# One decoder layer with a product-key expert mixer on one core: slot sums, one-hots and projection order changed

## The chip, the cores and the metric

The program runs on one core of a Trainium2 chip, in one launch. The metric is the device time of that launch in microseconds (us). An engine is named as the profile names it: TensorE is PE (matmuls) and PEld (its weight loads), VectorE is DVE, ScalarE is ACT, GpSimd is POOL, and SyncE (SP) only issues transfers.

## What is computed

The layer runs on 1024 prompt tokens and 64 sample tokens of width 1024, all in float32. Tokens lie in tiles of 128 rows: tiles 0 to 7 are the prompt, tile 8 (64 rows) is the sample group. Gating and retention heads, a cross-attention into 256 memory tokens and the expert mixer follow one another, each with a residual and a layer norm. The mixer is what the change is about, cut here to its core:

```python
q = (xt @ wq).reshape(128, 8, 2, 128)                      # 8 heads, two halves
s = einsum('thcd,hckd->thck', q, subkeys)                  # 128 keys per half
sv, si = top_k(s, 16)
cand = sv[:, :, 0, :, None] + sv[:, :, 1, None, :]         # 256 candidates per head
fv, fi = top_k(cand, 16)                                   # 8 x 16 = 128 experts per token
g = softmax(fv)
act = gelu(einsum('thed,td->the', u_tab[eidx], xt))
f = einsum('the,thed->td', g * act, v_tab[eidx])           # tables of 16384 x 1024
```

## The kernel before

**Two ways through the mixer.** Tiles 1, 2, 3, 4 (`DT`) go the dense way: every expert of the tables is projected for them, in 128 blocks of 128 experts, and a table of weights that is zero nearly everywhere picks the chosen ones. Tiles 0, 8, 5, 6, 7 (`GT`) go by gathers: POOL issues one indirect transfer for each of the 128 slots of a tile (L1154, L1157), which brings one row of 1024 numbers for each of up to 128 partitions into `gbuf` (7 buffers).

**Gathers.** The list `jobs` is written from `JORD`: `u` is a slot whose rows of the first table are dotted with the tokens by DVE (L1087), into one column of `hd`. The values come in two forms. In form `v` a gather fetches the 128 rows of one token, and PE sums them with 32-column matmuls into `cb` (L1128): two matmuls for a gather, four records in the profile. In form `w` a gather fetches one slot for all tokens, and DVE adds it, scaled by a column of `hd`, to the sum `fo` (L1099). Before the change only tile 7, which is last, has form `w`; tile 0 is first in the list and has form `v`.

**The front.** `front()` sends four batches of tiles ([0], [1, 2, 8], [3, 4, 5], [6, 7]) through the projections; all of their large matmuls are L148, into `mm`. While PE projects for one batch, the route of the batch before (`post_peer`) selects its experts, mostly on DVE (L617 to L661). For a tile of the dense way the selection ends in 32 groups of one-hots (`onehots`): `oi` marks one half index (DVE, L705), `oj` the other one, already times the weight (ACT, L702 and L703, two instructions for each of 4 rows), PE multiplies the two (`gb`, L719), ACT copies the product into the one buffer `big` (L720), and after every fourth group SP stores it to `gsc` in DRAM (L723). One tile at a time does this.

**The dense part.** `do_h(i)` projects block i (24 matmuls, L973), ACT takes the gelu (L977), DVE multiplies by the stored table `G` (L980), and hi and lo parts go to `ah` and `al`. Then 48 matmuls for two blocks (L1024) add their values `vh`, `vl` into `oa` to `od`. The first two blocks are projected while the last selections still run; then the pools of the selection close (`qctx.close()`), two pools for values and sums open in their place, and the rest follows.

**What sets the order.** Two generators, the front with the dense part and the gathers, each have a clock that its yields advance; the one that is behind is asked next, and its clock gives its instructions their priority. A scheduler then fixes one order for each engine, which the chip follows strictly: an instruction that waits holds up all that stand behind it on its engine, a transfer on SP's or POOL's queue too.

Of the kernel before, what the change touches and what calls it, by code (L numbers as in the profile page):

```python
# [13 lines left out]
AF = mybir.ActivationFunctionType  # L14
ALU = mybir.AluOpType
# [39 lines left out]
SPREAD = (0,1,2,3)  # L55
HEAD = "w_o w_o + wq wq + wo wo + pq pq + pq pq + +"
PIN = 1
PO = 0
PG = 0
PC = 0  # L60
PP = 0
# [7 lines left out]
ND = 2  # L69
GT = [0,8,5,6,7]  # L70
DT = [1,2,3,4]
JORD = ("u0","v0","u8","v8","u5","v5a","u6 v5b","u7 v6","w7")
FB = 2
COST_G = 1.4
COST_F = 1.1
# [83 lines left out]
def body(ctx: ExitStack, tc: tile.TileContext, a):  # L159
    nc = tc.nc  # L160
# [40 lines left out]
    iota = C("iota")  # L201
# [58 lines left out]
    def pin(x, PIN=1):  # L260
        if not PIN:
            return
        n = 0
        for i in reversed(nc.cur_bb.bb.instructions):
            if i is not x.ins and i.engine == x.ins.engine and i.name not in low:
                n += 1
                if n == PIN:
                    tc.add_manual_dep(x.ins, i.name, mybir.DependencyInfo(mybir.DependencyClass.NoSync,
                                                                          mybir.DependencyReason.DATA), reason="order")
                    return  # L270
# [317 lines left out]
    def post_peer(t, c, p, sub):  # L588
# [26 lines left out]
        for j in range(4):  # L615
            x = s[:P, j * 128:(j + 1) * 128]
# [68 lines left out]
        if c == 3 and dn:  # L685
            while st.get("gsl") or not st.get("gok"):
                yield
            st["gsl"] = True
            tp = GB()
            for j, src in enumerate((eid[:, 0, :], eid[:, 1, :], gw)):  # L690
                nc.tensor.transpose(tp[:, j * 128:(j + 1) * 128], src, ident)
            kt = TQ([128, 5, 128], "kt", 1)
            tpv = tp[:, :384].rearrange("p (a b) -> p a b", a=3)
            nc.scalar.activation(kt[:, :3, :], tpv, AF.Copy)
            nc.scalar.activation(kt[:, 3:5, :], tpv[:, 1:3, :], AF.Copy, scale=-1.0)
            yield
            n = DT.index(t)

            def onehots(g):
                oj = TQ([128, 4, 128], "oj", OJ)  # L700
                for r in range(4 * g, 4 * g + 4):
                    nc.scalar.activation(oj[:, r % 4, :], iota, AF.Abs, bias=kt[:, 3, r:r + 1])  # L702
                    nc.scalar.activation(oj[:, r % 4, :], oj[:, r % 4, :], AF.Relu, bias=kt[:, 2, r:r + 1], scale=kt[:, 4, r:r + 1])  # L703
                oi = TQ([128, 4, 128], "oi", OI)
                x = nc.vector.tensor_tensor(oi, iota.unsqueeze(1).to_broadcast([128, 4, 128]),  # L705
                                            kt[:, 0, 4 * g:4 * g + 4].unsqueeze(2).to_broadcast([128, 4, 128]), op=ALU.is_equal)
                pin(x, PO)
                return oi, oj

            nxt = onehots(0)  # L710
            for g in range(32):
                if g % 4 == 0:
                    gs = TQ([128, 128, 16], "big")
                oi, oj = nxt
                if g < 31:
                    nxt = onehots(g + 1)
                g4 = GB()
                for r in range(4):
                    nc.tensor.matmul(g4[:, r * 128:(r + 1) * 128], lhsT=oj[:, r, :], rhs=oi[:, r, :], start=True, stop=True)  # L719
                nc.scalar.activation(gs[:, :, g % 4 * 4:g % 4 * 4 + 4].rearrange("p i t -> p t i"),  # L720
                                     g4.rearrange("p (t i) -> p t i", t=4), AF.Copy)
                if g % 4 == 3:
                    nc.sync.dma_start(gsc[8 * n + g // 4], gs)  # L723
                if g % 2:
                    yield
            st["gsl"] = False
        elif c == 3:
            tp = GB() if XG else SM()
            nc.tensor.transpose(tp[:, :P], eid[:P, 0, :], ident[:P, :P])
            nc.vector.tensor_copy(done["ixT", t][:, :P], tp[:, :P])  # L730
            done["v", t] = True
            if t == SMP:
                for x in (done["ix", t], gw):
                    nc.sync.dma_start(x[64:, :64], x[:64, 64:])
                done["u", t, 3] = True
# [166 lines left out]
    def dense():  # L902
# [6 lines left out]
        def TE(shape, tag, bufs=1, dt=F32):  # L909
            return pe[0].tile(shape, dt, name=tag, tag=tag, bufs=bufs)  # L910
# [10 lines left out]
        NB = 128  # L921
# [3 lines left out]
        def load_u(i):  # L925
            if i < NB:
                raw["u", i] = TD([128, 8, 128], "ur", ND)
                nc.sync.dma_start(raw["u", i], a["Ud"][i])

        def load_v(i):  # L930
            if i < NB:
                raw["v", i] = TE([128, 1024], "vr", ND)
                nc.sync.dma_start(raw["v", i], a["V"][i * 128:(i + 1) * 128, :])

        def load_g(q):
# [6 lines left out]
        def split_u(i):  # L942
            if i < NB:
                h, l = TD([128, 8, 128], "uh", 2, F32R), TD([128, 8, 128], "ul", 2, F32R)
                split(h, l, raw.pop(("u", i)))
                Uw[i] = (h, l)
                load_u(i + ND)
# [13 lines left out]
            del r  # L961
        for i in range(ND):
            load_u(i)
        split_u(0)
        split_u(1)
        A = {}

        def do_h(i):
            h, l = Uw.pop(i)
            p = pp.tile([128, nd * 128], F32, name="h", tag="h", bufs=2)  # L970
            for k in range(8):
                for j, (w, x) in enumerate(((h, xh), (h, xl), (l, xh))):
                    nc.tensor.matmul(p, lhsT=w[:, k, :], rhs=x[:, k, :], start=k == 0 and j == 0, stop=k == 7 and j == 2)  # L973
                if k % 2 and k < 7:
                    yield 1.35
            ga = TD([128, nd * 128], "ga", 2)
            nc.scalar.activation(ga, p, AF.Gelu_apprx_tanh)  # L977
            gv = ga.rearrange("p (h g t) -> p h g t", h=2, t=16)
            for j in range(2):
                nc.vector.tensor_tensor(gv[:, j], gv[:, j], Gb[i // 8, j][:, :, i % 8, :], op=ALU.mult)  # L980
            ah, al = TD([128, nd * 128], "ah", 2 * FB, F32R), TD([128, nd * 128], "al", 2 * FB, F32R)
            split(ah, al, ga)
            A[i] = (ah, al)
            if i % 8 == 7:
                del Gb[i // 8, 0], Gb[i // 8, 1]
                load_g(i // 8 + 1)
# [2 lines left out]
            step_all()  # L989
            yield 1.0  # L990
        load_g(0)
        for i in range(FB):
            yield from do_h(i)
            split_u(i + 2)
            step_all()
            yield 1.35
        while active:
# [2 lines left out]
        qctx.close()  # L1000
        pe = [ctx.enter_context(tc.tile_pool(name="pe", bufs=1, side="right")),
              ctx.enter_context(tc.tile_pool(name="po", bufs=1, space=bass.MemoryType.PSUM, side="right"))]
        for i in range(ND):
            load_v(i)
        for t in DT:
            y = TE([128, 1024], "acc", nd)
            nc.sync.dma_start(y, done["x2", t])
# [2 lines left out]
            split_v(i)  # L1010
        phase[0] = 2
        for f in range(NB // FB):
            for i in range((f + 1) * FB, (f + 2) * FB):
                if i < NB:
                    yield from do_h(i)
                    split_u(i + 2)
                    yield 1.35
            for n, t in enumerate(DT):
                o = [O(2 * (n % 2) + j) for j in range(2)]
                for b in range(FB):  # L1020
                    i = f * FB + b
                    for ia, iv in ((0, 0), (0, 1), (1, 0)):
                        for j in range(2):
                            nc.tensor.matmul(o[j], lhsT=A[i][ia][:, n * 128:(n + 1) * 128],  # L1024
                                             rhs=Vw[i][iv][:, j * 512:(j + 1) * 512],
                                             start=b == 0 and ia + iv == 0, stop=b == FB - 1 and ia == 1)
                    if b < FB - 1:
                        yield 1.4
                for j in range(2):
                    y = acc[n][:, j * 512:(j + 1) * 512]  # L1030
                    nc.vector.scalar_tensor_tensor(y, y, ALPHA if f == 0 else 1.0, o[j], op0=ALU.mult, op1=ALU.add)
                if f == NB // FB - 1:
                    if n == 0:
                        lg, lb = TE([128, 1024], "vr", ND), TE([128, 1024], "vr", ND)
                        nc.sync.dma_start(lg, bc(a["ln3_g"], 1024))
                        nc.sync.dma_start(lb, bc(a["ln3_b"], 1024))
                    finish(acc[n], t, lg, lb)
                if n == nd - 1:
                    for b in range(FB):
                        del A[f * FB + b], Vw[f * FB + b]  # L1040
                        split_v((f + 1) * FB + b)
                yield 1.4

    def main():
        yield from front()
# [192 lines left out]
```

## Time and profile before

| | |
|---|---|
| median of 3 runs | 3679.9 us (3675.48 to 3682.37) |
| the profiled execution | 3672.27 us, span 3670.5 us |
| mean granted TensorE clock | 0.931 of full speed |
| busy share | PE 88%, PEld 56%, DVE 68%, ACT 35%, POOL 49% |
| chain that ended last | PE 63%, DVE 13%, DMA 9% |
| first and last `h` matmul start | 2044.1 us, 3630.2 us |

The shares are means over stretches that differ. The front ends and the dense part begins at about 2044 us; the rows below go by stretches, cut where PE passes from one part of the front to the next.

### The profile page before, as it was taken

The page shows a single profiled execution, that of the slowest core. Times are in us where ns is not written, and L with a number is a line of the kernel's source. Part 1 is how long each engine was busy: PE and PEld are TensorE (multiplying, and loading weights), DVE is VectorE, ACT ScalarE, POOL GpSimd, SP SyncE. Part 2 cuts the span into 40 slices and gives each one's busy share as a digit, 9 for nine tenths or more (in the row PEclk, how much of TensorE's full clock was granted, in tenths as well). Part 3 has the DMA queues.
Part 4 walks back from the last instruction along what each step waited for, and adds up shares of the span by engine and source line. Part 5 has one row for each costly group of instructions (what it writes and reads, how often), then busy time and mean ns, then how long its engine had stood idle before and what let it go on. Part 6 is the DMA issues. An engine that isn't in the chain of part 4 may idle for free.

```text
span 3670.5 us, 41634 instructions
## 1 busy us (share of the span) xinstructions
PE 3244.9 (88%) x13368; PEld 2037.7 (56%) x13368; DVE 2496.5 (68%) x5941; ACT 1274.3 (35%) x2634; POOL 1784.9 (49%) x1427
## 2 busy tenths in 40 slices
PE   8999558889997899984789779999999999999998
PEld 3444223333445554442445467777777777788886
DVE  2135874325678622799858769878877777799996
ACT  1121211112238785231677932222322322322222
POOL 0013575234546633446744546555565655566631
PEclk9989679899998899986889889999999999999999
DMA  8747677778768887667888879988999989898872
GB/s 271 258 158 275 214 285 278 253 268 283 269 235 330 309 307 283 210 235 263 300 308 313 305 275 338 327 306 316 337 332 347 343 317 324 298 322 318 309 239 75
DMA packets 407354, 1039.67 MB, mean 283 GB/s; under 512 B 37280, under 2 KB 129632, under 8 KB 403040
## 3 DMA queue, kind: packets, MB, share of 16 engines
q0 software_dynamic: 165888, 604.05, 45.3%
q1 hardware_dynamic: 229392, 420.06, 33.5%
q10 hardware_dynamic: 11856, 12.91, 1.0%
q8 instruction: 105, 1.72, 0.2%
q14 instruction: 113, 0.93, 0.1%
HBM read 985.59 MB, written 51.25 MB: 282 GB/s over the span
## 4 chain that ended last, share of the span: by engine, by line
PE 63%; DVE 13%; DMA 9%; POOL 5%; issue 5%; ACT 5%; SPq 0%; POOLq 0%; DVEq 0%; ACTq 0%
PE mm L148 20%; PE h L973 15%; PE cb L1128 5%; PE oa L1024 4%; PE oc L1024 4%; PE od L1024 4%; PE ob L1024 4%; DVE gbuf L1087 4%; DMA gbuf<-in_U_dram,ix 3%; POOL gbuf L1154 2%; PE gb L719 2%; DMA gbuf<-in_V_dram,ixT 2%; DMA ret<-in_cv_dram 1%; ACT oj L702 1%; ACT oj L703 1%
## 5 line engine op out<-in xcount | busy, mean ns | idle before, releaser
L148 PE MATMUL mm<-wr,aT 128*128 128x512 f32 (+1 forms) x2432 | 1126.5, 611 | 34.2 <-DMA aT<-in_xpT_dram 19.0
L1154 POOL DMA_INDIRECT gbuf<-in_U_dram,ix x576 | 711.8, 1236 | 540.7 <-DVE hd L1087 340.2
L1087 DVE CUSTOM_DVE_ANT_0 gbuf<-gbuf,x2g 128x1024 f32<-128x1024 f32 x576 | 733.6, 1287 | 239.7 <-DMA gbuf<-in_U_dram,ix 207.2
L1157 POOL DMA_INDIRECT gbuf<-in_V_dram,ixT x448 | 493.8, 1102 | 568.7 <-PE cb L1128 323.9
L148 PEld LDWEIGHTS mm<-wr,aT 128*128 128x128 f32 (+1 forms) x2432 | 439.2, 190 | 586.0 <-issue 524.2
L973 PE MATMUL h<-x,uh 128*128 128x512 f32 x2048 | 644.3, 392 | 0.8 <-ACT uh L917 0.8
L973 PEld LDWEIGHTS h<-x,uh 128*128 128x128 f32 x2048 | 385.8, 189 | 91.9 <-issue 6.7
L973 PE MATMUL h<-x,ul 128*128 128x512 f32 x1024 | 401.6, 392 | 3.3 <-DVE ul L918 3.3
L917 ACT ACTIVATE vh<-vr 128x1024 fp32r<-128x1024 f32 x128 | 134.9, 1061 | 491.4 <-PE od L1024 487.6
L1128 PE MATMUL cb<-gbuf,Z 128*32 128x512 f32 x1792 | 242.8, 636 | 20.4 <-DMA gbuf<-in_V_dram,ixT 20.3
L1154 POOL DMA_INDIRECT gbuf<-in_V_dram,ix x128 | 182.4, 1425 | 123.6 <-DVE fo L1099 97.8
L917 ACT ACTIVATE ah<-ga 128x512 fp32r<-128x512 f32 x128 | 80.8, 632 | 454.4 <-DVE ga L980 438.7
L719 PE MATMUL gb<-oi,oj 128*128 128x128 f32 x1024 | 168.8, 312 | 68.7 <-ACT big L720 37.9
L918 POOL TENSOR_TENSOR vl<-vr,vh 128x1024 fp32r<-128x1024 f32 x64 | 159.9, 2499 | 130.6 <-ACT vh L917 91.5
L719 PEld LDWEIGHTS gb<-oi,oj 128*128 128x128 f32 x1024 | 151.7, 218 | 127.0 <-ACT oj L703 43.7
L973 PEld LDWEIGHTS h<-x,ul 128*128 128x128 f32 x1024 | 193.0, 188 | 50.0 <-issue 5.0
L703 ACT ACTIVATE oj<-oj,kt 128x128 f32<-128x128 f32 x512 | 215.0, 483 | 0.0
L1099 DVE SCALAR_TENSOR_TENSOR fo<-gbuf,hd,fo 128x1024 f32<-128x1024 f32 x127 | 184.9, 1456 | 1.2
L917 ACT ACTIVATE uh<-ur 128x1024 fp32r<-128x1024 f32 x128 | 134.8, 1054 | 122.5 <-PE h L973 115.7
L705 DVE TENSOR_TENSOR oi<-cst,kt 128x512 f32<-128x512 f32 x128 | 88.9, 700 | 129.4 <-PE gb L719 128.0
L660 POOL TENSOR_TENSOR cd<-cd,sif 128x512 f32<-128x512 f32 (+1 forms) x72 | 105.5, 1478 | 144.4 <-DVE cd L658 134.0
L918 DVE TENSOR_TENSOR ul<-ur,uh 128x1024 fp32r<-128x1024 f32 x128 | 161.8, 1264 | 14.8 <-ACT uh L917 14.7
(232 smaller groups left out, 5102.1 us busy)
## 6 DMA issues: line engine op xcount, KB each, us to landing
ur<-in_Ud_dram SPq DMA_DIRECT2D x128, 512.0 KB, 7.0
vr<-in_V_dram SPq DMA_DIRECT2D x128, 512.0 KB, 5.8
wr<-in_w_in_dram SPq DMA_DIRECT2D x192, 256.0 KB, 5.2
wr<-in_pq_dram SPq DMA_DIRECT2D x128, 256.0 KB, 5.4
gsc<-big SPq DMA_DIRECT2D x32, 1024.0 KB, 6.9
G<-gsc SPq DMA_DIRECT2D x32, 1024.0 KB, 17.9
wr<-in_w_o_dram SPq DMA_DIRECT2D x64, 256.0 KB, 4.9
wr<-in_wq_dram SPq DMA_DIRECT2D x64, 256.0 KB, 6.4
```

The source lines that it names most:

```text
L148: self.nc.tensor.matmul(p, lhsT=lT(k), rhs=w, start=k == 0, stop=k == KB - 1)
L703: nc.scalar.activation(oj[:, r % 4, :], oj[:, r % 4, :], AF.Relu, bias=kt[:, 2, r:r + 1], scale=kt[:, 4, r:r + 1])
L719: nc.tensor.matmul(g4[:, r * 128:(r + 1) * 128], lhsT=oj[:, r, :], rhs=oi[:, r, :], start=True, stop=True)
L917: nc.scalar.activation(hi, raw, AF.Copy)
L918: eng.tensor_tensor(lo, raw, hi.bitcast(F32), op=ALU.subtract)
L973: nc.tensor.matmul(p, lhsT=w[:, k, :], rhs=x[:, k, :], start=k == 0 and j == 0, stop=k == 7 and j == 2)
L1024: nc.tensor.matmul(o[j], lhsT=A[i][ia][:, n * 128:(n + 1) * 128], rhs=Vw[i][iv][:, j * 512:(j + 1) * 512], start=b == 0 and ia + iv == 0, ...
L1087: dot = nc.vector.tensor_tensor_reduce(out=g, in0=g, in1=x2s[t], scale=1.0, scalar=0.0, op0=ALU.mult, op1=ALU.add, accum_out=hd[t][:, i:i ...
L1099: dot = nc.vector.scalar_tensor_tensor(fo[t], g, hd[t][:, i:i + 1], fo[t], op0=ALU.mult, op1=ALU.add)
L1128: nc.tensor.matmul(comb[t][q:q + 32, :], lhsT=Z[:, z + 4 * c1 + r1 % 4, 31 - r1:63 - r1], rhs=g1[:, n * 512:(n + 1) * 512], start=r1 == VQ ...
L1154: nc.gpsimd.indirect_dma_start(out=g, out_offset=None, in_=a["U" if kind == "u" else "V"], in_offset=bass.IndirectOffsetOnAxis(ap=done["ix ...
L1157: nc.gpsimd.indirect_dma_start(out=g, out_offset=None, in_=a["V"], in_offset=bass.IndirectOffsetOnAxis(ap=done["ixT", t][:, i:i + 1], axis=0))
```

## The change

The string `JORD` gives tile 0 the form `w`. In every second group of one-hots (odd g) `oj` becomes a plain one-hot made by DVE in one instruction of 128x512, and POOL multiplies `oi` by the weights; even groups are as before, but `oi` is written first. The first `FB` projections ahead of the pools' change become `2 * FB`, so that in the loop a group of projections follows the sums rather than leading them; the raw values `vr` move to a pool that is open from the start, and the first two are loaded there. The sequence of projections and sums in the loop is otherwise the same.

```diff
-JORD = ("u0","v0","u8","v8","u5","v5a","u6 v5b","u7 v6","w7")
+JORD = ("u0","w0","u8","v8","u5","v5a","u6 v5b","u7 v6","w7")
...
             def onehots(g):
                 oj = TQ([128, 4, 128], "oj", OJ)
-                for r in range(4 * g, 4 * g + 4):
-                    nc.scalar.activation(oj[:, r % 4, :], iota, AF.Abs, bias=kt[:, 3, r:r + 1])
-                    nc.scalar.activation(oj[:, r % 4, :], oj[:, r % 4, :], AF.Relu, bias=kt[:, 2, r:r + 1], scale=kt[:, 4, r:r + 1])
                 oi = TQ([128, 4, 128], "oi", OI)
...
+                nc.vector.tensor_tensor(oi, iota.unsqueeze(1).to_broadcast([128, 4, 128]), over(0), op=ALU.is_equal)
+                if g % 2:
+                    nc.vector.tensor_tensor(oj, iota.unsqueeze(1).to_broadcast([128, 4, 128]), over(1), op=ALU.is_equal)
+                    nc.gpsimd.tensor_tensor(oi, oi, over(2), op=ALU.mult)
+                else:
+                    for r in range(4 * g, 4 * g + 4):
+                        nc.scalar.activation(oj[:, r % 4, :], iota, AF.Abs, bias=kt[:, 3, r:r + 1])
...
-                raw["v", i] = TE([128, 1024], "vr", ND)
+                raw["v", i] = TD([128, 1024], "vr", ND)
...
         for i in range(ND):
             load_u(i)
+            load_v(i)
...
-        for i in range(FB):
+        for i in range(2 * FB):
             yield from do_h(i)
...
-        for i in range(ND):
-            load_v(i)
...
         for f in range(NB // FB):
-            for i in range((f + 1) * FB, (f + 2) * FB):
-                if i < NB:
-                    yield from do_h(i)
-                    split_u(i + 2)
-                    yield 1.35
...
+            for i in range((f + 2) * FB, (f + 3) * FB):
+                if i < NB:
+                    yield from do_h(i)
+                    split_u(i + 2)
+                    yield 1.35
```

Three places of the order show what moved. The first is DVE in the front, in the selection of a tile of the second batch (`sv`, `si` and `cd` are its scores). Before:

```order
L617 MAX sv<-ps 128x8 x4
L619 MAX_INDEX si<-sv,ps 128x8 x4
L620 MATCH_REPLACE ps<-sv,ps 128x128 x4
L621 MAX sv<-ps 128x8 x4
L622 MAX_INDEX si<-sv,ps 128x8 x2
L1121 COPY Z<-wT 128x8
L622 MAX_INDEX si<-sv,ps 128x8
```

and with the change:

```order
L616 MAX sv<-ps 128x8 x4
L341 SCALAR_TENSOR_TENSOR ret<-th,ret 128x128
L1104 SCALAR_TENSOR_TENSOR fo<-gbuf,hd,fo 128x1024
L340 TENSOR_TENSOR ret<-ret,rt 128x2x64 x2
L618 MAX_INDEX si<-sv,ps 128x8 x4
L1104 SCALAR_TENSOR_TENSOR fo<-gbuf,hd,fo 128x1024
L337 TENSOR_TENSOR rt<-ret,rot 128x256
L619 MATCH_REPLACE ps<-sv,ps 128x128 x4
L1104 SCALAR_TENSOR_TENSOR fo<-gbuf,hd,fo 128x1024
L337 TENSOR_TENSOR ret<-ret,rot 128x256
L620 MAX sv<-ps 128x8 x4
L1104 SCALAR_TENSOR_TENSOR fo<-gbuf,hd,fo 128x1024
```

The sums of tile 0 (L1104 is L1099 of before) now stand one by one between the steps of the selection and of the retention heads, where a small copy of the matmul form stood now and then. By this order 14 of the 128 come before the last layer-norm step of the second batch, 34 before the step that lay at 824 us in the trace of before, and all 128 before the first dot of tile 8.

The second is PE where the third batch passes from its input projection to its output projection; `nat` is what the transposes wait for. Before:

```order
L384 MATMUL sm<-ret 128x128
L719 MATMUL gb<-oi,oj 128x128 x4
L317 MATMUL sm<-g_7001,wsT 128x128 x2
L719 MATMUL gb<-oi,oj 128x128 x4
L317 MATMUL sm<-g_7077,wsT 128x128 x2
L719 MATMUL gb<-oi,oj 128x128 x10
L317 MATMUL sm<-g_7149,wsT 128x128
L296 MATMUL sm<-cst,nat 128x128
```

and with the change:

```order
L383 MATMUL sm<-ret 128x128
L316 MATMUL sm<-g_6747,wsT 128x128 x2
L316 MATMUL sm<-g_6817,wsT 128x128 x2
L690 MATMUL gb<-cst,eid 128x128 x2
L690 MATMUL gb<-cst,gwd 128x128
L725 MATMUL gb<-oi,oj 128x128 x5
L316 MATMUL sm<-g_6883,wsT 128x128
L295 MATMUL sm<-cst,nat 128x128
```

From the last matmul of the input projection to the first of the output projection 45 one-hot matmuls stood in PE's order, now 12; with 8 that stood just before, ten groups have moved behind the beginning of the output projection. By DVE's order 23 of the 64 dots of tile 8 (L1087) have moved back as well, past the layer norm that follows.

The third is SP's queue at the pools' change. Before:

```order
L723 DMA gsc<-big 128x2048 x3
L939 DMA G<-gsc 128x16x128
L933 DMA vr<-in_V_dram 128x1024 x2
L1007 DMA acc<-x2d_3786 128x1024
```

and with the change:

```order
L965 DMA ur<-x2T_79 128x1024
L939 DMA vr<-in_V_dram 128x1024 x2
L945 DMA G<-gsc 128x16x128
L729 DMA gsc<-big 128x2048
```

The first two blocks of values are loaded before the last stores of the table rather than behind them. On PE four blocks of `h` stand ahead of the first `oa` in the order of before as well as in the new one.

## Rows read from the trace of the kernel before

**Rows 1.** Windows by stretch; busy us of each engine (instructions), granted clock, DMA share, GB/s:
```profile
736.00:824.00 88.00, 72.97 (x261) 27.80 (x261) 21.95 (x53) 12.79 (x25) 35.29 (x36) 0.90 0.78 264
824.00:1048.00 224.00, 216.82 (x848) 90.15 (x850) 136.46 (x720) 54.55 (x147) 110.51 (x112) 0.98 0.79 273
1048.00:1200.00 152.00, 127.46 (x518) 73.82 (x518) 121.85 (x406) 106.44 (x269) 90.76 (x76) 0.89 0.79 294
1200.00:1483.00 283.00, 258.17 (x1196) 144.06 (x1196) 109.43 (x209) 203.23 (x490) 112.63 (x104) 0.95 0.82 293
1483.00:1800.00 317.00, 220.66 (x676) 117.11 (x675) 295.75 (x1120) 88.92 (x237) 169.27 (x139) 0.82 0.70 246
1800.00:1935.00 135.00, 111.90 (x522) 69.14 (x521) 75.82 (x153) 103.52 (x254) 71.71 (x61) 0.91 0.86 315
1935.00:2054.00 119.00, 99.80 (x491) 54.20 (x490) 104.45 (x504) 95.36 (x252) 64.11 (x57) 0.91 0.86 309
2054.00:2142.00 88.00, 55.60 (x273) 41.29 (x271) 39.54 (x84) 72.17 (x168) 31.63 (x26) 0.73 0.75 268
2142.00:3670.00 1528.00, 1496.49 (x6801) 1152.39 (x6801) 1260.66 (x1769) 414.44 (x522) 853.30 (x624) 0.99 0.85 303
```

**Rows 2.** The same view for line L1128 alone (PE, PEld):
```profile
736.00:824.00 88.00, 16.63 (x112) 3.28 (x112) 0.90 0.78 264
824.00:1048.00 224.00, 41.31 (x324) 8.74 (x328) 0.98 0.79 273
1048.00:1100.00 52.00, 11.01 (x80) 2.20 (x80) 0.97 0.63 216
```

**Rows 3.** Single lines; duration ns min/median/max, first and last start us:
```profile
L1099 DVE SCALAR_TENSOR_TENSOR fo<-gbuf,hd,fo x127: 1269/1277/3847, 3205.1 to 3553.9; 128x1024 f32<-128x1024 f32 x127
L705 DVE TENSOR_TENSOR oi<-cst,kt x128: 637/688/2253, 1089.0 to 2119.7; 128x512 f32<-128x512 f32 x128
L660 POOL TENSOR_TENSOR cd<-cd,sif x72: 1253/1286/2575, 313.3 to 2065.1; 128x512 f32<-128x512 f32 x64, 64x512 f32<-64x512 f32 x8
```

**Rows 4.** Groups by line, DVE, 824 to 1048 us; busy us, mean ns, idle before:
```profile
L1121 DVE COPY Z<-wT 128x8 f32<-128x8 f32 x10 | 6.0, 604 | 16.0 <-PE cb L1128 16.0
```

**Rows 5.** Timeline of DVE, then POOL, near 1695 us; start us, duration us:
```profile
1694.68 1.21 DVE L1087 CUSTOM_DVE_ANT_0 gbuf<-gbuf,x2g 128x1024 f32<-128x1024 f32 x1
1695.82 2.28 DVE L1087 CUSTOM_DVE_ANT_0 gbuf<-gbuf,x2g 128x1024 f32<-128x1024 f32 x1
...
1694.85 2.17 POOL L660 TENSOR_TENSOR cd<-cd,sif 128x512 f32<-128x512 f32 x1 [0.31 <-DVE mv_r L282]
```

**Rows 6.** PE's timeline between the third batch's input and output projections:
```profile
1101.19 1.88 PE L148 MATMUL mm<-wr,aT 128*128 128x512 f32 x4
...
1114.74 4.15 PE L719 MATMUL gb<-oi,oj 128*128 128x128 f32 x16 [2.46 <-ACT oj L703]
...
1141.48 3.60 PE L719 MATMUL gb<-oi,oj 128*128 128x128 f32 x16 [5.44 <-ACT big L720]
...
1150.20 1.99 PE L148 MATMUL mm<-wr,aT 128*128 128x512 f32 x4
```

**Rows 7.** Groups by line, ACT, 2054 to 2142 us; busy us, mean ns, idle before:
```profile
L703 ACT ACTIVATE oj<-oj,kt 128x128 f32<-128x128 f32 x64 | 27.1, 480 | 0.0
L702 ACT ACTIVATE oj<-cst,kt 128x128 f32<-128x128 f32 x64 | 20.5, 385 | 0.0
L720 ACT ACTIVATE big<-gb 128x512 f32<-128x512 f32 x18 | 18.2, 1042 | 3.8 <-PE gb L719 1.9 <-DMA gsc<-big 1.7
```

**Rows 8.** The chain that ended last, 2000 to 2200 us; start us, us, what:
```profile
2115.33 6.57 DMA gsc<-big
...
2129.53 3.83 DMA gsc<-big
2133.44 5.96 DMA G<-gsc
2139.88 0.86 ACT ah L917 x2
2140.94 1.05 ACT vh L917
2142.03 0.80 PE oa L1024
```

**Rows 9.** Waits of PE, 1935 to 2054 us; us in total, times, longest:
```profile
PE gb L719 <- ACT big L720: 6.9, 1, 6.9
```

More of the change, by code (lines that the diff above doesn't have):

```diff
@@ L57 @@
 PIN = 1
-PO = 0
 PG = 0
@@ L700, in onehots, with over @@
                 oj = TQ([128, 4, 128], "oj", OJ)
-                for r in range(4 * g, 4 * g + 4):
-                    nc.scalar.activation(oj[:, r % 4, :], iota, AF.Abs, bias=kt[:, 3, r:r + 1])
-                    nc.scalar.activation(oj[:, r % 4, :], oj[:, r % 4, :], AF.Relu, bias=kt[:, 2, r:r + 1], scale=kt[:, 4, r:r + 1])
                 oi = TQ([128, 4, 128], "oi", OI)
-                x = nc.vector.tensor_tensor(oi, iota.unsqueeze(1).to_broadcast([128, 4, 128]),
-                                            kt[:, 0, 4 * g:4 * g + 4].unsqueeze(2).to_broadcast([128, 4, 128]), op=ALU.is_equal)
-                pin(x, PO)
+                def over(w):
+                    return kt[:, w, 4 * g:4 * g + 4].unsqueeze(2).to_broadcast([128, 4, 128])
+                nc.vector.tensor_tensor(oi, iota.unsqueeze(1).to_broadcast([128, 4, 128]), over(0), op=ALU.is_equal)
[5 more added lines that the diff above has]
+                        nc.scalar.activation(oj[:, r % 4, :], iota, AF.Abs, bias=kt[:, 3, r:r + 1])
+                        nc.scalar.activation(oj[:, r % 4, :], oj[:, r % 4, :], AF.Relu, bias=kt[:, 2, r:r + 1],
+                                             scale=kt[:, 4, r:r + 1])
                 return oi, oj
@@ L1033, in dense @@
                     if n == 0:
-                        lg, lb = TE([128, 1024], "vr", ND), TE([128, 1024], "vr", ND)
+                        lg, lb = TD([128, 1024], "vr", ND), TD([128, 1024], "vr", ND)
                         nc.sync.dma_start(lg, bc(a["ln3_g"], 1024))
```

## The prediction

> **What bounds the kernel now.** I read the windows by stretch first [rows 1]. From 2142 us on PE is busy for 1496 of 1528 us at nearly full clock: the dense part is PE's, and nothing of its sequence changes, by the order. So the change is won or lost ahead of it, and the first eight stretches say where. From 824 to 1048 us PE is the bound (217 of 224 us) while DVE works 136 us. From 1048 to 1200 us nobody is: PE stops for 49 us between two projections, and its idle gaps there end with ACT's one-hots and copies [rows 6]. From 1483 to 1800 us DVE is the bound, 296 of 317 us, and PE falls to 221 us at a granted clock of 0.82. That stretch shows how full DVE gets when it is the bound: 0.93. From 2054 to 2142 us ACT works 72 of 88 us, most of it on one-hots [rows 7], and PE waits.
>
> Every term below is set against the profiled execution, 3672.3 us with a span of 3670.5. It lies 7.6 us under the median of the runs, 3679.9.
>
> **1. Sums of tile 0 on DVE, 736 to 1048 us.** PE loses the matmuls of the `v` form: 16.6 + 41.3 + 11.0 = 69 us [rows 2]. DVE gains 128 sums. Their nearest row is the same instruction for tile 7, median 1277 ns [rows 3], so 163 us.
>
> From 736 to 824 us DVE is idle for 66 us [rows 1], and 34 sums (43 us) fit. But 14 of them, 18 us, stand in DVE's order ahead of the layer norm that the next projection waits for. Half of that falls into gaps, I take it: 9 us late, against some 4 us that PE gains, as the rest of its 16.6 us is freed while it waits anyway. **+5**; ends -17 (all PE work gone on the path) and +18 (all sums on the path).
>
> From 824 to 1048 us the other 94 sums stand between the steps of the selections, and all of them ahead of tile 8. DVE then has 136.5 - 6.0 (the copies for the matmul form [rows 4]) + 94 x 1.277 = 250.5 us. To this comes a lock: a dot that begins while POOL multiplies takes 2.28 in place of 1.21 us, and POOL's multiply 2.17 [rows 5] in place of 1.29 [rows 3], so the two take turns. At most 1.07 us for each of the 18 multiplies in this stretch, 19 us; I take half, 9. DVE needs 260 us, at a fill of 0.93 279 us, where 224 went by. PE needs only 217 - 41 = 176 us and follows, because it has few buffers ahead of DVE. **+55**; ends +26 (no lock, fill 1) and +66 (full lock).
>
> PE's clock will drop in this stretch as it did from 1483 to 1800 us. At 0.82 in place of 0.98 its 176 us become 210, still covered by DVE's 279.
>
> **2. One-hots, tiles 1 and 2, 1048 to 1483 us.** A group costs ACT (27.1 + 20.5)/16 + 1.04 = 4.0 us [rows 7]. By the order ten groups no longer stand between the two projections of the third batch, 40 us of ACT's work there, and 23 dots have left DVE. PE's gap of 49 us [rows 6] shrinks by nearly that: **-38**; ends -49 and 0. The ten groups come after 1200 us, where PE is the bound, 258 of 283 us. Each is 8 matmul records; 16 of them took 3.6 us in the slow gap [rows 6], so half that at full clock, 9 us; a PE wait or two for ACT goes. **+8**; ends 0 and +20. DVE's new compares and POOL's multiplies are covered in that stretch, DVE having 109 of 283 us.
>
> **3. One-hots, tiles 3 and 4, 1800 to 2142 us.** In each odd group ACT loses 3.0 us, DVE gains a compare, 0.69 us [rows 3], and POOL a multiply like L660, 1.29 us. From 1800 to 1935 us no engine is full: **-2**, ends -6 and +10. From 1935 to 2054 us DVE is at 104.5 of 119, and by the order 12 of the new compares and multiplies fall here. That is 12 x 0.69 = 8.3, and the lock at 0.8 us of its 1.07 (DVE is busy 88% of the time), 9.6: DVE has 122.4 us, at 0.93 132 us, +13. Half of PE's wait for ACT's copy, 6.9 us [rows 9], goes: **+9**; ends -7 and +20. From 2054 us on 16 groups remain, and half of the 47.6 us of their `oj` work is gone. What binds then is the single buffer `big`: four copies of 1.04 and a store of 6.57 us [rows 8] are 10.7 us for four groups, where 14.2 lie between two stores now. Four times 3.5 is 14, less something for multiplies queued behind gathers on POOL: **-12**; ends -24 and 0.
>
> **4. Four blocks ahead.** The order already had four blocks of `h` ahead of the first sum, so the first half of this edit does nothing. The values come sooner, but the chain there goes over the last store, the table's load and `ah` [rows 8]; only `vh`'s 1.05 us after `ah` can go. **-1**; ends -2 and 0.
>
> SP gets the two value loads ahead of the table's stores and POOL the same number of gathers for tile 0 as before, so neither queue is a term.
>
> The sum: 5 + 55 - 38 + 8 - 2 + 9 - 12 - 1 = **+24 us**, 3696 us against the profiled execution, **3704 us** against the median.
>
> **A rule that speaks against the multiplies.** The trace shows a POOL multiply of 128x512 at 1286 ns and a DVE compare of that size at 688 [rows 3], and the two engines taking turns [rows 5]. The Trainium skill's page "GPSIMD Engine Reference", section 8 (Key points), says that DVE is about twice as fast at elementwise work, and that POOL shares its SBUF interfaces with VectorE and contends with DVE instructions that read two SBUF inputs. It names no size for this contention. Taken as a slowing that hides in gaps, the locks of my sum, 19 us, are nil and the sum is +4 us; taken as whole turns it is +24. The rows show whole turns, so I keep +24.
>
> **Rivals.**
> *Faster: the sums fit into DVE's gaps.* From 736 to 1048 us DVE is idle for 312 - 158 = 154 us [rows 1], and the sums less the copies need 157. If the scheduler's order lets them fall into gaps across both stretches, so that DVE is full without anything behind it being late, the two stretches cost +10 in place of +60: -26 us, **3654**. For it: the balance fits nearly exactly, and 34 sums stand early. Against it: the order gives 94 of them to a stretch with only 88 us of gaps. It decides itself by whether PE stays above 90% busy there.
>
> *A wash.* The ends of two gains are reached, -49 in the gap and -24 at the switch, and pay for DVE's stretch: 24 - 11 - 12 = +1, **3681**. For it: ACT is what PE waits for in both places.
>
> *Slower by far: the lock weighs fully.* DVE fills only to 0.85 in its stretch, as gathers and multiplies wait for each other on POOL's queue (260/0.85 = 306, +27 more), and the 32 multiplies after 1800 us cost 1.07 each with none covered (34 in place of 10, +24): 24 + 51 = +75, **3755**. For it: POOL already works half of that stretch. Against it: a fill of 0.93 with dots and gathers in it has been seen.
>
> *The change does not do what it says.* For the fourth part this is what I expect, and it is in the sum.
>
> **How the numbers follow.** Forecast 0.49, faster rival 0.27, wash 0.14, far slower 0.10. The likeliest case's own range is 3680 to 3735, from the ends of the terms of DVE's stretch and the gap. The range that should hold 8 in 10 goes from the faster rival with 9 us of its gains' ends to the far slower one: 3645 to 3755. About 0.2%, 7 us, is what a measurement of this kernel can tell from no change. Faster than that: the faster rival and a little of the wash, 0.29. Within: most of the wash and the edge of the forecast, 0.13. Slower: 0.58.
>
> **What would show it.** In the new profile the stretch from tile 0's first sum to tile 8's first dot should show DVE above 90% and PE near 65%, with a granted clock near 0.8, and last some 55 us longer. The gap between the third batch's projections should be some 10 us, not 49. The last 16 groups should take some 45 us with ACT no longer full, and the first `oa` should come 20 to 30 us later than 2142. If PE stays above 90% through the sums, or the first `oa` comes earlier than 2142, the central step, that DVE becomes the bound between 824 and 1048 us, is wrong.

## The result and the profile after

The changed kernel takes 3699.5 us (median of 5 runs, 3693.0 to 3703.3); the kernel before, on the same chip, 3675.5 us (5 runs, 3673.6 to 3682.4). The ratio is 1.006, with an interval of 1.0046 to 1.0075: slower by 24 us (22 by the ratio). That is the forecast sum (its 3704 us stood against a median of 3679.9 for the kernel before), and still two of its large terms were wrong for PE and cancelled, as the profile shows.

The profiled execution took 3701.03 us (span 3699.3, mean granted clock 0.916). These are its windows by stretch, with the columns of [rows 1], cut where the same instructions of DVE stand in the trace before and after (their order in between differs, so a stretch doesn't hold quite the same work):

```profile
736.00:826.00 90.00, 56.99 (x137) 24.83 (x136) 62.16 (x79) 11.85 (x23) 57.33 (x43) 0.77 0.87 304
826.00:1111.00 285.00, 219.91 (x635) 105.10 (x634) 245.99 (x815) 59.16 (x156) 153.47 (x116) 0.88 0.68 236
1111.00:1217.00 106.00, 73.63 (x252) 42.80 (x251) 94.39 (x342) 45.43 (x115) 47.78 (x44) 0.79 0.45 165
1217.00:1498.00 281.00, 253.41 (x1177) 151.34 (x1176) 169.25 (x298) 162.46 (x353) 166.97 (x146) 0.93 0.89 323
1498.00:1824.00 326.00, 244.53 (x790) 128.09 (x789) 298.64 (x1122) 88.38 (x231) 191.78 (x153) 0.83 0.75 268
1824.00:1959.00 135.00, 111.31 (x514) 70.71 (x514) 87.67 (x159) 71.36 (x157) 83.07 (x70) 0.91 0.86 311
1959.00:2086.00 127.00, 106.32 (x581) 68.54 (x580) 116.84 (x513) 82.77 (x200) 74.14 (x64) 0.93 0.84 300
2086.00:2165.00 79.00, 41.41 (x205) 23.66 (x203) 50.93 (x100) 39.63 (x83) 51.82 (x43) 0.67 0.84 299
2165.00:3699.00 1534.00, 1496.52 (x6785) 1153.42 (x6785) 1257.08 (x1765) 414.58 (x523) 854.19 (x621) 0.99 0.85 301
```

The second row is the stretch of the sums: 285 us where 224 went by, DVE 86% busy, PE 77% at a granted clock of 0.88. The third is 46 us shorter than before, with the DMA share down from 0.79 to 0.45. At the switch (2086 to 2165 us) ACT, which had 72 of 88 us, now has 40 of 79. The dense part has the same work and takes 1534 us for 1528.

The sums, and the compares and multiplies of the odd groups, as single lines (duration ns min/median/max, first and last start us):

```profile
L1104 DVE SCALAR_TENSOR_TENSOR fo<-gbuf,hd,fo x254: 1221/1275/3212, 739.7 to 3576.3; 128x1024 f32<-128x1024 f32 x127
L707 DVE TENSOR_TENSOR oj<-cst,kt x64: 672/683/2158, 1158.0 to 2140.0; 128x512 f32<-128x512 f32 x64
L708 POOL TENSOR_TENSOR oi<-oi,kt x64: 1040/1058/2775, 1158.2 to 2145.9; 128x512 f32<-128x512 f32 x64
```

**The stop between the third batch's projections** is read apart. The windows view of it before (47.6 us between two projection matmuls, the same columns):

```profile
1102.60:1150.20 47.60, 28.21 (x126) 23.85 (x124) 40.11 (x110) 47.41 (x120) 33.64 (x28) 0.68 0.75 274
```

The same stop after, 48.3 us:

```profile
1119.50:1167.80 48.30, 16.53 (x78) 14.27 (x77) 47.23 (x231) 21.80 (x60) 14.74 (x15) 0.58 0.08 25
```

And the waits of PE in it after (us in total, times, longest):

```profile
PE sm L345 <- DVE ret L340: 15.3, 1, 15.3
PE gb L725 <- DVE abf L650: 5.2, 1, 5.2
PE gb L690 <- DVE mv_g L281: 4.3, 1, 4.3
PE sm L316 <- ACT on L287: 4.1, 2, 3.8
```

ACT was full in the stop before and is at 45% now, and the stop is as long. DVE works through it: 47.2 of 48.3 us. PE had 90 records of one-hot matmuls there (two for each matmul), now 24. So it isn't ACT that sets the length now; DVE has work of the same length. The groups of DVE in the stop say which. Two of them before:

```profile
L1087 DVE CUSTOM_DVE_ANT_0 gbuf<-gbuf,x2g 128x1024 f32<-128x1024 f32 x14 | 17.0, 1217 | 0.2 <-DMA gbuf<-in_U_dram,ix 0.2
L658 DVE TENSOR_TENSOR cd<-abf,cst 64x512 f32<-64x512 f32 x2 | 1.3, 676 | 0.0
```

And two after:

```profile
L657 DVE TENSOR_TENSOR cd<-abf,cst 128x512 f32<-128x512 f32 (+1 forms) x6 | 3.8, 682 | 0.0
L618 DVE FIND_INDEX8 si<-sv,ps 128x8 uint32<-128x128 f32 (+1 forms) x8 | 2.2, 275 | 0.0
```

The dots of tile 8 are gone from it, and selection steps stand there that the kernel before had done ahead of the stop: it has no step of `si` in its stop. The lateness of DVE's selections, of which PE had felt 16.9 us ahead of the stop, is worked off here. That is read from the rows; no run separates it.

The next table gives what the argument below rests on: how much later than before PE reaches a place, in the profiled executions. A place is the first or last projection matmul at one of PE's long stops. The kernels of the other columns come in the next section.

| PE reaches (before, us) | after | sums alone | one-hots alone | fourth part alone | one-hots + fourth | half the sums | sums in two halves |
|---|---|---|---|---|---|---|---|
| end of third input projection, 1102.6 | +16.9 | +18.8 | +3.6 | +1.6 | +7.8 | -30.4 | -25.3 |
| start of its output projection, 1150.2 | +17.6 | +18.4 | +24.3 | +1.7 | +29.1 | -28.8 | -11.6 |
| the stop between them, 47.6 long | 48.3 | 47.3 | 68.2 | 47.7 | 68.9 | 49.2 | 61.3 |
| next batch, 1422.0 | +5.1 | +12.1 | +19.8 | +4.5 | +26.8 | -41.3 | -33.4 |
| 1695.9 | +31.1 | +26.8 | +11.3 | +3.8 | +19.1 | -34.0 | -29.4 |
| first `oa`, 2142.0 | +22.9 | +18.2 | +4.6 | +13.6 | +16.0 | -33.2 | -55.9 |
| span, 3670.5 | +28.8 | +17.1 | +11.3 | +10.6 | +23.5 | -36.0 | -42.0 |

One profiled execution is good to about 10 us in this table: a kernel whose order is the old one up to 2050 us ("one-hots late", below) was 11.0 us late at 1150.2.

### The profile page after: what moved, and what is told of

It reads as the page before. It is cut to its first block, busy times and chain, and to the rows that moved or that the text cites. A ratio compares the mean times of both kernels' runs of the same rounds, so it can differ in the third digit from the quotient of the medians.

```text
span 3699.3 us, 40523 instructions
## 1 busy us (share of the span) xinstructions
PE 3193.8 (86%) x12855; PEld 2039.1 (55%) x12855; DVE 2714.9 (73%) x6116; ACT 1098.6 (30%) x2112; POOL 1929.7 (52%) x1491
## 4 chain that ended last, share of the span: by engine, by line
PE 35%; DVE 9%; DMA 6%; issue 4%; POOL 3%; ACT 1%; POOLq 0%; SPq 0%; DVEq 0%; ACTq 0%
PE h L980 14%; PE oa L1024 4%; PE oc L1024 4%; PE od L1024 4%; PE ob L1024 4%; DMA gbuf<-in_U_dram,ix 3%; DVE gbuf L1092 3%; PE cb L1133 2%; POOL gbuf L1159 2%; PE mm L147 1%; DMA gsc<-big 1%; DMA gbuf<-in_V_dram,ixT 1%; POOL gbuf L1162 1%; PE gb L725 1%; ACT big L726 0%
## 5 line engine op out<-in xcount | busy, mean ns | idle before, releaser
L1159 POOL DMA_INDIRECT gbuf<-in_U_dram,ix x576 | 731.7, 1270 | 505.7 <-DVE hd L1092 324.2
L1092 DVE CUSTOM_DVE_ANT_0 gbuf<-gbuf,x2g 128x1024 f32<-128x1024 f32 x576 | 756.6, 1327 | 241.3 <-DMA gbuf<-in_U_dram,ix 211.4
L1162 POOL DMA_INDIRECT gbuf<-in_V_dram,ixT x320 | 364.1, 1138 | 339.2 <-DVE hd L1092 153.3
L1159 POOL DMA_INDIRECT gbuf<-in_V_dram,ix x256 | 355.7, 1389 | 259.1 <-DVE fo L1104 132.9
L1104 DVE SCALAR_TENSOR_TENSOR fo<-gbuf,hd,fo 128x1024 f32<-128x1024 f32 x254 | 353.1, 1390 | 19.7 <-DMA gbuf<-in_V_dram,ix 18.3
L1133 PE MATMUL cb<-gbuf,Z 128*32 128x512 f32 x1280 | 165.5, 627 | 20.9 <-DMA gbuf<-in_V_dram,ixT 20.8
L726 ACT ACTIVATE big<-gb 128x512 f32<-128x512 f32 x128 | 130.2, 1050 | 112.0 <-PE gb L725 93.7
```

Of the source, the lines that this page charges most:

```text
L1092: dot = nc.vector.tensor_tensor_reduce(out=g, in0=g, in1=x2s[t], scale=1.0, scalar=0.0, op0=ALU.mult, op1=ALU.add, accum_out=hd[t][:, i:i ...
L1104: dot = nc.vector.scalar_tensor_tensor(fo[t], g, hd[t][:, i:i + 1], fo[t], op0=ALU.mult, op1=ALU.add)
L1133: nc.tensor.matmul(comb[t][q:q + 32, :], lhsT=Z[:, z + 4 * c1 + r1 % 4, 31 - r1:63 - r1], rhs=g1[:, n * 512:(n + 1) * 512], start=r1 == VQ ...
L1159: nc.gpsimd.indirect_dma_start(out=g, out_offset=None, in_=a["U" if kind == "u" else "V"], in_offset=bass.IndirectOffsetOnAxis(ap=done["ix ...
L1162: nc.gpsimd.indirect_dma_start(out=g, out_offset=None, in_=a["V"], in_offset=bass.IndirectOffsetOnAxis(ap=done["ixT", t][:, i:i + 1], axis=0))
```

## The experiments

**Sums alone.** The kernel before with the change's first edit only.

```diff
-JORD = ("u0","v0","u8", ...)
+JORD = ("u0","w0","u8", ...)
```

> The kernel before with tile 0's sums on VectorE and nothing else. Theory (VectorE becomes the bound between 824 and 1048 us, the gap between the third batch's projections empties because the one-hots are ordered behind it): the last sum comes near 1110 us as in the changed kernel, the gap of 49 us shrinks although ACT makes all one-hots, and the total is +25 to +40 us over the kernel before. Rival (the gap shrinks because of the cheaper one-hots, as the prediction had it): the gap stays and the total is +55 us or more. Rival (the sums fit into gaps): within 10 us of the kernel before, or faster.

Measured: 3700.0 us, ratio 1.0081 (1.0064 to 1.0098), some 30 us slower: alone the sums cost at least as much as the whole change. In its stop only 16 one-hot records are left, and ACT still makes all `oj`. The time is in the theory's range, but the stop does not shrink: it is 47.3 us. So with the sums its length doesn't hang on ACT's one-hots, and what moves them out of it are the sums, not the edit of the one-hots. Whether ACT set the length in the kernel before, where it was full too, no run separates.

**One-hots alone.** The odd groups' `oj` and weights on DVE and POOL, and `oi` written first in every group as in the change; the rest as before.

```diff
+if g % 2:
+    nc.vector.tensor_tensor(oj, iota..., over(1), op=ALU.is_equal)
+    nc.gpsimd.tensor_tensor(oi, oi, over(2), op=ALU.mult)
+else:
     (ACT, as before)
```

> The kernel before with the one-hots of odd groups on VectorE and POOL and nothing else. The order puts 16 groups into the gap between the third batch's projections where the kernel before had 11. Theory (the gap's gain belongs to the sums' delay, the one-hots only relieve ACT there and in the last 16 groups): -5 to -20 us. Rival (the prediction's split, gain of the gap and of the switch are both the one-hots'): -40 us or more. Rival (POOL's multiplies lock VectorE and make PE wait for oi): 0 to +15 us.

Measured: 3687.5 us, ratio 1.0049 (1.0031 to 1.0067): slower by 18 us, a miss, nearest to the second rival. Here the order puts 128 one-hot records into the stop, and it is 68.2 us long. Waits of PE in it:

```profile
PE gb L726 <- POOL oi L709: 11.9, 5, 3.3
PE gb L736 <- DVE eid L666: 11.5, 1, 11.5
PE gb L726 <- ACT big L727: 5.0, 2, 4.1
```

More groups are put ahead of the projection, and there PE waits longest for POOL's multiplies, and once for a DVE step. At the other end the gain is there: DVE's steps are 25 us late at 2032 us and 4 us at 2149.

**Fourth part alone.** Value rows loaded ahead, four blocks ahead.

```diff
-raw["v", i] = TE([128, 1024], "vr", ND)
+raw["v", i] = TD([128, 1024], "vr", ND)
 for i in range(ND):
     load_u(i)
+    load_v(i)
...
-for i in range(FB):
+for i in range(2 * FB):
     yield from do_h(i)
```

> The kernel before with four blocks ahead and the values loaded early, and nothing else. Theory (four blocks were ahead already, only vh's 1 us can go): within 5 us of the kernel before. Rival (early loads shorten the start of the dense part, where PE waited 12 us for vh): -8 to -12 us.

Measured: 3682.9 us, ratio 1.003 (1.0018 to 1.0041): 11 us, where I had put nothing. In the trace it is lost at the switch. Of PE's waits between 2100 and 2300 us the longest is that of the first `oa` for `ah` (the longest behind the switch in the kernel before is 12.3 us, for `vh`):

```profile
PE oa L1018 <- ACT ah L917: 19.2, 1, 19.2
```

In DVE's order three dots of the next tile stand ahead of the first product with the full table, and of DVE's waits between 2135 and 2160 us the longest are theirs, for gathers:

```profile
DVE gbuf L1086 <- DMA gbuf<-in_U_dram,ix: 10.5, 2, 6.4
```

**One-hots and fourth part, without the sums.** The changed kernel with `"v0"` in place of `"w0"`.

> The changed kernel with tile 0's values in the matmul form again. Theory: the sum of the second and third experiment, -5 to -20 us against the kernel before, so 30 to 45 us under the changed kernel. Rival (the one-hots' lock costs what ACT's relief gives): equal to the kernel before.

Measured: 3692.6 us, ratio 1.0048 (1.0031 to 1.0065), a miss as well. The parts don't add: 30, 18 and 11 us alone, 18 for the last two together, 22 for all three (by the ratios). With the sums most of the one-hots stand behind the stop, and it stays at 48.3 us, not 68.9.

**Half the sums.** The changed kernel without every second value sum of tile 0, so that half of that tile's values are missing.

```diff
+elif t == 0 and i % 2 and i < P - 1:
+    dot = None
```

> The changed kernel, but every second value sum of tile 0 (63 of its 127 fused sums on DVE) is left out; its gathers and buffers stay. So half of tile 0's value sum is missing from the output. Theory (DVE is the bound between tile 0's first sum and tile 8's first dot): the stretch that came out 62 us late loses about 46 sums of 1.28 us, so it is only 5 to 20 us late; the stop between the third batch's projections then gives back less (28 one-hot matmuls stand in it instead of 12), so that the whole comes out 8 to 20 us under the changed kernel's 3699: 3679 to 3691. Rival (the gathers, which wait for their turn on POOL's queue, set the pace of that stretch): it stays 50 us or more late and the time stays within 4 us of 3699.

Measured: 3640.9 us, ratio 0.991 (0.9891 to 0.9929): by the ratios some 55 us under the changed kernel, far more than the theory's 8 to 20. The stretch of the sums in its windows:

```profile
821.00:1048.00 227.00, 200.26 (x576) 94.45 (x575) 191.77 (x756) 53.51 (x149) 141.20 (x119) 0.92 0.81 294
```

It takes 227 us, not 285, with DVE at 84%: as predicted, the number of sums decides this stretch, and the gathers, which all stay, don't. The failed part of the expectation is that the stop would take much of it back. It stays 49.2 us, and PE keeps what it won.

**Value loads alone, blocks alone.** The two halves of the fourth part, each on the kernel before.

```diff
 (value loads)  TE -> TD for "vr", load_v(i) behind load_u(i); blocks as before
 (blocks)       range(FB) -> range(2 * FB), later blocks two groups ahead; loads as before
```

> The kernel before with only the first half of the fourth part: the value rows' buffers and their first two loads ahead of the front's end; the blocks stay two ahead in the text. Theory (the cost of the fourth part is the new order on DVE at the switch: three dots of the next tile, each waiting for its gather, stand ahead of the first product of the activations with the full table, where none stood before): two such dots stand there in this kernel, so about 2/3 of the fourth part's 9 to 11 us, 3678 to 3683. Rival 1 (the value loads on SP's queue and their transfers are what delays the last stores): the whole of it here, 3682 to 3686, and nothing in the kernel with the blocks alone. Rival 2 (the four blocks' own order is the cost): nothing here, 3672 to 3676.

> The kernel before with only the second half of the fourth part: four blocks ahead of the first sum in the text and the later blocks two groups ahead; the value rows' loads stay behind the front's end. Theory (dots ahead of the first full product on DVE): two of them stand there in this kernel too, 3678 to 3683. Rival 1 (the value loads): nothing, 3672 to 3676. Rival 2 (the blocks' order): the whole of it, 3682 to 3686.

Measured: value loads 3704.8 us, ratio 1.0082 (1.0064 to 1.0101); blocks 3678.0 us, ratio 1.0001 (0.999 to 1.0012). My theory of the dots falls: two of them stand ahead of the first product in the blocks' kernel and it costs nothing. It is the value loads' edit, as rival 1 had it in kind, but at 30 us, and the blocks take 19 of them back. That edit moves the buffers to another pool and loads them sooner; no run separates the two. In the value loads' kernel PE is behind right after the switch. Its windows from 2142 to 2300 us, then those of the kernel before:

```profile
2142.00:2300.00 158.00, 140.67 (x631) 107.41 (x632) 124.26 (x189) 42.91 (x57) 90.83 (x66) 0.94 0.89 314
```

```profile
2142.00:2300.00 158.00, 156.13 (x712) 118.56 (x712) 138.76 (x205) 42.20 (x54) 102.44 (x72) 0.99 0.93 329
```

But most of this was carried in: PE starts its first `oa` 14.8 us late in this execution, and 10.5 of them were there at 1899 us, where its order on DVE and POOL is still the old one; the blocks' kernel was as late there. The other 15 of the 30.1 us by which its span is longer come in the dense part, where PE's waits for DVE's `acc` are 12.9 us in place of 6.8 and those for gathered values 9.2 in place of 5.8. Which queue or buffer passes this on to PE I did not settle.

**One-hots late.** As one-hots alone, but with the odd groups' new form only in the second half of the last dense tile.

```diff
-if g % 2:
+if g % 2 and n == 3 and g > 15:
```

> The kernel before with the one-hots of odd groups on DVE and POOL only in the second half of the last dense tile, 8 groups of 128. Everything ahead of about 2050 us is ordered as before, and no dot stands ahead of the first full product on DVE. Theory (ACT's one-hots are what PE and the stores wait for in the last 16 groups, and the one-hots cost time everywhere else): the 21 us that the odd one-hots gained between 2032 and 2150 us are kept without their cost, 3655 to 3667. Rival (the single buffer of 16 rows and its store of 6.6 us set that stretch, and the 21 us were only lateness from before that would have been lost in a wait anyway): 3670 to 3677.

Measured: 3671.7 us, ratio 0.9988 (0.9977 to 1.0): a gain of some 4 us at the edge of what can be told. The time lies in the rival's range, not in the theory's. Its chain at the switch reads as the one before [rows 8] from the last store on:

```profile
2129.60 3.83 DMA gsc<-big
2133.52 5.92 DMA G<-gsc
2139.46 0.44 DVE ga L987
2139.91 0.82 ACT ah L924 x2
2140.97 1.05 ACT vh L924
2142.06 0.79 PE oa L1031
```

It gets there on time although this execution was 10.6 us late at 2069, so ACT's relief in the last groups may be worth some 10 us in this trace, not 21. For it: the blocks' kernel, with the one-hots of before, was 10.5 us late at 1899 and still 10.7 at its first `oa`. The rest of the 21 I take for lateness caught up in waits; no run shows it.

**Multiplies on DVE.** The changed kernel with `nc.vector` for the odd groups' multiply.

```diff
-nc.gpsimd.tensor_tensor(oi, oi, over(2), op=ALU.mult)
+nc.vector.tensor_tensor(oi, oi, over(2), op=ALU.mult)
```

> The changed kernel with the 64 multiplies of the odd groups' weights on DVE instead of POOL. Theory (POOL's multiplies cost by their length and by the turns they take with DVE): up to 1.07 us of turn for each of 64 go, as does most of PE's 18.5 us of waits for them, against 64 x 0.7 = 45 us more on DVE, half of it where DVE has room: 3685 to 3696. Rival (what counts is DVE's load, the turns hide): 3702 to 3720.

Measured: 3706.7 us, ratio 1.0088 (1.0066 to 1.011), no better than the change and probably some 7 us worse (the intervals overlap), as the rival had it. The multiply itself, as a single line:

```profile
L708 DVE TENSOR_TENSOR oi<-oi,kt x64: 639/684/1747, 1159.7 to 2134.7; 128x512 f32<-128x512 f32 x64
```

So the multiplies cost no less on DVE, 64 x 0.68 = 44 us of it, than on POOL with its turns. What the turns cost by themselves this run doesn't show.

**Sums in two halves.** The kernel before with slots 0 to 63 of tile 0 behind its dots, the rest behind the dots of tile 8.

```diff
-JORD = ("u0","v0","u8","v8", ...)
+JORD = ("u0","w0a","u8","w0b","v8", ...)
```

> The kernel before with tile 0's value rows summed by slot on DVE as in the change, but in two halves: slots 0 to 63 right behind tile 0's dots, slots 64 to 127 behind the dots of tile 8; one-hots and the fourth part as before. Theory (the sums cost because 94 of them crowd into one stretch in which DVE has 88 us to spare; taken out of PE they are worth some 60 us): the first half fits as in the kernel with half the sums left out, the second half's 64 x 1.28 = 82 us fall where DVE works 109 of 283 us, so most of the 36 us by which that kernel beat the kernel before are kept: 3637 to 3662. Rival (the second half only moves the crowding: its sums stand in DVE's order ahead of the layer norms of the next batch, and the later gathers push the next tiles back): 3672 to 3700.

Measured: 3630.8 us, ratio 0.989 (0.9866 to 0.9914): some 40 us faster than before, better than the theory's range. Its windows of the sums' first stretch, and of the stretch that answers to 1483 to 1800 us before:

```profile
829.00:1040.00 211.00, 186.96 (x542) 88.41 (x541) 166.12 (x741) 51.30 (x144) 64.71 (x54) 0.94 0.43 144
...
1449.00:1719.00 270.00, 221.61 (x848) 106.96 (x846) 218.96 (x994) 83.90 (x228) 151.21 (x139) 0.89 0.81 284
```

The first stretch is 13 us shorter than before; DVE, 79% busy, has room for its sums. The second is 47 us shorter, and not through the sums: the second half's gathers push the dots of tile 5 back, as the rival said, but out of the stretch in which DVE was the bound. In the groups of DVE there, 34 dots are left:

```profile
L1087 DVE CUSTOM_DVE_ANT_0 gbuf<-gbuf,x2g 128x1024 f32<-128x1024 f32 x34 | 43.8, 1296 | 6.0 <-DMA gbuf<-in_U_dram,ix 5.8
```

The kernel before has 96 in its stretch:

```profile
L1087 DVE CUSTOM_DVE_ANT_0 gbuf<-gbuf,x2g 128x1024 f32<-128x1024 f32 x96 | 122.4, 1285 | 6.6 <-DMA gbuf<-in_U_dram,ix 6.6
```

PE is 55.9 us early at its first `oa`. Of these, 14 us are lost again in the dense part of this execution; the cause of that stays open.

**Both gains; the change with its sums in two halves.** The first is the kernel just shown with the one-hots late; the second the changed kernel with `"w0a"`, `"u8"`, `"w0b"`.

> The kernel with the sums in two halves (slots 0 to 63 behind tile 0's dots, 64 to 127 behind tile 8's), and also the one-hots of odd groups on DVE and POOL in the second half of the last dense tile alone. Theory (the two gains lie in different stretches, so they add: 44 us and 5 us): 3622 to 3631. Rival (the last 16 groups are no longer bound by ACT once the front comes earlier): 3630 to 3636.

> The changed kernel with tile 0's sums in two halves, slots 0 to 63 behind tile 0's dots, 64 to 127 behind tile 8's, and all else as in the change. Theory (the place of the second half of the sums is what made the change slower; the one-hots of all odd groups and the fourth part cost some 10 to 18 us on their own): under the kernel before by 25 to 40 us, 3635 to 3650, and 5 to 20 us over the kernel with the split sums alone. Rival (with DVE relieved in the crowded stretch the one-hots on DVE and POOL pay): 3615 to 3630.

Measured: 3623.0 us, ratio 0.9861 (0.9839 to 0.9883), and 3650.6 us, ratio 0.9933 (0.9914 to 0.9952). The first is the fastest kernel of this study, 51 us under the kernel before by the ratio; its interval overlaps that of the split sums alone, so the late one-hots' share is not clear of noise. The second shows that the place of the sums is what turned the change: with it mended the change is 20 us faster than before (the edge of its range), and its one-hots and fourth part still cost some 16 to 20 us beside the split sums alone.

## Why the prediction was right, step by step

The forecast, +24 us with the sums making DVE the bound, came out; the chance for slower was the larger one. Of its signs, the length of DVE's stretch (61 us more, where some 55 was said) and the first `oa` (22.9 us later, 20 to 30) came. DVE's share there (86%, above 90%), PE's (77%, near 65%) and the clock (0.88, near 0.8) came weaker than said, and the stop of some 10 us not at all: it is 48.3. Its terms, with PE's lateness from the table and DVE's from the windows:

- **Before 824 us: +5.** DVE's step at 824 us came 2.3 us late. Right.
- **The sums, 824 to 1048 us: +55.** DVE was 62 us late at the end of the stretch, so its own part of the step holds in sum: 246 us busy at a fill of 0.86, where I had 260 at 0.93. The fill is the one of the rival that was slower by far (0.85). The load is smaller since only 14 of the 18 `cd` steps of the selections (L658, now L657) stand in the stretch, not because the sums were cheaper. The step that failed is that PE "follows, because it has few buffers ahead of DVE". PE ended the third input projection only 16.9 us late, less than the 60 us of the first two terms by 43. It lost 69 us of matmuls, and DVE's late selections were not what its projection needed next; they come in the stop. Half the sums put the same place 30.4 us *early*: that the number of DVE's sums sets the time there is shown by the runs.
- **The stop: -38.** The failed step is "PE's gap of 49 us [rows 6] shrinks by nearly that": I took the waits for ACT that end its idle gaps for its length. It went from 47.6 to 48.3 us. The two errors, 43 and 39 us, cancel, and by the rows they hang together: the selections that PE didn't wait for ahead of the stop fill DVE in it. DVE's own third stretch is 46 us shorter, near the term, but with 24 dots (28 us of DVE) and 11 compares fewer in it, not by ACT's work.
- **After 1200 us: +8.** PE went from +17.6 at 1150 to +31.1 at 1696, so +13.5. The size was near, the place was not: at 1422 PE was only 5.1 us late, and by DVE's windows the stretch up to 1483 took 281 us for 283 and the next, for which I had nothing, 326 for 317. The late groups stand at that seam: of the 64 compares `oi` of tiles 1 and 2, the groups of DVE show 22 between 1400 and 1557 us, where the kernel before had 5 between 1400 and 1523. There PE is busy for 93 of 98 us (1400 to 1498) and then for 58 of 59.
- **1800 to 1935, to 2054, and to the switch: -2, +9, -12, -1.** DVE's steps were 24 us late at 1800 and 1935, 33 us at 2032, and the first `oa` 22.9: 0, +9 and -10. Right. The chain at the switch after:

```profile
2117.00 9.19 DMA gsc<-big
...
2145.91 1.06 POOL oi L708
2147.01 2.09 PE gb L725 x8
2149.13 1.03 ACT big L726
2150.18 7.59 DMA gsc<-big
2157.83 5.97 DMA G<-gsc
2164.96 0.79 PE oa L1024
```

ACT's `oj` is 7.9% of it between 2086 and 2165 us, where it was 39.0% between 2054 and 2142 in the kernel before. Stores of 9.2 and 7.6 us, and a POOL multiply with gathers ahead of it on POOL from 2135.8 to 2145.1 us, take its place, which is why the term gained 10 us and didn't reach its end of 24.

- **Four blocks ahead: -1.** Alone it is +11, and the value loads by themselves +30, where I had said that "neither queue is a term". In the change the dense part behind the first `oa` is 6 us longer, but I can't say whether that is from this; the cost by itself was missed, since I looked at PE's order and not at what early loads do on the way.

Attribution was the weak side: I gave the one-hots -35 us (-38, +8, -2, +9 and -12), and alone they are 18 us slower. That the total is right to the microsecond is luck, the sum of errors that cancel, not precision.

**The turns of POOL and DVE.** The forecast allowed 9 us for them in the sums' stretch. In the groups there 95 sums took 133.0 us:

```profile
L1104 DVE SCALAR_TENSOR_TENSOR fo<-gbuf,hd,fo 128x1024 f32<-128x1024 f32 x95 | 133.0, 1400 | 0.0
```

That is 1400 ns for one against a median of 1275, 95 x 0.125 = 12 us, near enough. The cause is in the timelines: 17 of the sums overlap a POOL multiply of 128x512 and take 2.01 us on average, the other 77 that begin in the stretch take 1.27, and every sum over 1.5 us is among the 17. One of them, with its multiply:

```profile
929.49 2.96 DVE L1104 SCALAR_TENSOR_TENSOR fo<-gbuf,hd,fo 128x1024 f32<-128x1024 f32 x1
...
930.08 1.27 POOL L659 TENSOR_TENSOR cd<-cd,sif 128x512 f32<-128x512 f32 x1
```

So the turns are real DVE time in the stretch where DVE is the bound, as the sum of +24 had it. The Trainium skill's page "GPSIMD Engine Reference", section 8 (Key points), has DVE about twice as fast at elementwise work; the same multiply took 1058 ns on POOL and 684 on DVE, a factor of 1.55. By that alone the multiplies would be better on DVE; the run with them there was no faster.

## What to carry to other kernels

An idle gap of one engine has more than one chain behind it: before a gap's wait is counted as a gain, look whether another engine is nearly full inside it. Work moved off a bound engine can pay once it is cut in pieces and put where the receiving engine has room. Here the same 128 sums cost 30 us in one place and won 40 us in two halves. And a moved job moves what queues behind it, which may be worth more than the job: the dots that the second half pushed out of DVE's crowded stretch were 62 of 96.

## What was unexpected of the hardware

POOL's multiply of 128x512 for the weights took 1058 ns, the one of the same size for the selections 1286 [rows 3]; I had priced both alike. And in the stop the DMA share fell from 0.75 to 0.08 (274 to 25 GB/s), as the first gather of tile 8 was issued only at 1182.3 us, when its indices had been made; what this cost by itself no run separates.
